# Shifting the sample caches from DRAM to DRAM in a hybrid attention layer

## The chip, the cores and the metric

The kernel runs on one core of one Trainium2 chip. The metric is device time in microseconds (us) of the whole program, as the median of its runs; lower is better. Work goes to PE (matrix products, PEld its weight loads), DVE, ACT and POOL (element-wise work), and to 16 DMA engines that move data between the core's SBUF and DRAM. DMAs are issued by two in-order instruction streams, those of SP and of ACT. ACT thus both computes and issues, and an issue that has to wait keeps all of ACT's later instructions waiting.

## The reference, cut to what matters

One inference step of a layer with three mixers (band attention A, gated delta rule B, memory attention C), a merge and a feed-forward part. Only mixer A and its caches are touched here:

```python
k_all = jnp.concatenate([cache_a_k[l], k_a], axis=1)     # 8 samples: 512 cached + 16 new keys
v_all = jnp.concatenate([cache_a_v[l], v_a], axis=1)
o_a = _band_attention(q_a, k_all, v_all, q_pos, k_pos, k_pos >= 0, a_rel_bias[l])
...
a_k_p.append(k_a[:, tp - keep_p:])    # prompt: the last 512 keys (and values) become the cache
a_k_s.append(k_all[:, tn:])           # samples: the cache moved on by 16, with the 16 new keys behind
a_v_s.append(v_all[:, tn:])
```

The sample caches hold 8 samples x 512 positions x 1024 channels in f32, 16 MB for keys and 16 MB for values. The output is almost all a copy: 496 of its 512 positions stand in the input, and 16 are new.

## The kernel before, in words

Phase A (about the first 1130 us) runs over 8 groups g of 128 channels (two heads). For each group `a_qk` projects queries and keys, `a_v` projects values (each as three chunks of 384 columns; PE, then evacuated by ACT, DVE and POOL), `a_prompt` does the band attention of the 1024 prompt frames as 4 blocks G x 2 heads h, `a_sample` that of the 8 samples in two halves hb, and `b_front` prepares mixer B. A scheduler with a simulated clock merges all of it into one list per engine, by dependences and priority, so PE alternates between projections (tile `ps`) and attention (`S`, `tb`, `od`).

The cache outputs were written as follows, all issued by ACT:

- `a_sample` loads a half's cached keys (`kb`, 1024 KB, one buffer) and values (`vb`, 1024 KB, two buffers) on SP, and from these same SBUF tiles ACT sends the shifted caches out: L450 `o_aks<-kb` (1024 KB, 128 partitions; the new keys had been copied behind the cached ones) and L451 `o_avs<-vb` (992 KB, partitions 4 to 127, thus 124 of them). Both have to wait for the load, and `kb` can't be loaded again until L450 has been sent.
- `a_v` sends the new values: L357 `o_avs<-vs`, 8 DMAs of 8 KB, one a sample, in a row.
- `a_qk` and `a_v` send the prompt caches, L317 `o_akp<-y` and L342/L344 `o_avp<-y`.

Completion is counted on 8 semaphores, called lanes below (DMAHW0 to DMAHW7 in the order rows), which go round over the DMAs of SP and ACT together. A DMA that takes a lane first waits until the DMA that had it last is complete, and that wait stands in the stream of the engine that issues it.

Of the kernel before, what the change touches and what calls it, by code (L numbers as in the profile page):

```python
# [19 lines left out]
P = 128  # L20
D = 1024
SEQ = 1024
DB = 8
DT = 16
# [4 lines left out]
MEM = 256  # L29
# [28 lines left out]
def run(g, n=-1):  # L58

    while n and next(g, g) is not g:  # L60
        n -= 1


class K:
# [219 lines left out]
    def a_qk(self, g, pool):  # L284
        nc, d, A = self.nc, self.d, self.A

        qs = [pool.tile([P, SEQ], F32R, name=f"qs{h}") for h in range(2)]
        kd = [pool.tile([P, SEQ], F32R, name=f"kd{h}") for h in range(2)]
        kl = A["kl"]
        kr = pool.tile([P, P], F32, name="kr", bufs=2)  # L290
        qb = A["qbs"][g % 2]
        A.update(qs=qs, kd=kd, krn=kr, qbn=qb)
        rows = [(slice(64 * h, 64 * h + 64), slice(64 - 64 * h, 128 - 64 * h)) for h in range(2)]

        def ev_q(c, p):
            n = slice(c * CW, min((c + 1) * CW, SEQ))
            w = n.stop - n.start
            for t, (r, o) in zip(qs, rows):
                nc.scalar.mul(t[r, n], p[r, :w], 0.125)
                nc.vector.scalar_tensor_tensor(t[o, n], p[r, :w], 0.125, t[r, n].bitcast(F32), op0=ALU.mult, op1=ALU.subtract)  # L300
            if c == 2:
                s = p[:, 256:384].rearrange("p (b i) -> p b i", b=DB)
                nc.scalar.mul(qb[0:64, :, 0:16], s[0:64], 0.125)
                nc.scalar.mul(qb[64:128, :, 16:32], s[64:128], 0.125)

        def ev_k(c, p):
            n = slice(c * CW, min((c + 1) * CW, SEQ))
            w = n.stop - n.start
            for t, low, (r, o) in zip(kd, kl, rows):
                nc.scalar.copy(t[r, n], p[r, :w])  # L310
                nc.vector.tensor_sub(low[r, n], p[r, :w], t[r, n].bitcast(F32))
                nc.gpsimd.tensor_copy(t[o, n], t[r, n].bitcast(F32))
            if c > 0:
                y = pool.tile([P, CW], F32, name="y", bufs=4)
                nc.scalar.copy(y, p)
                m = slice(128, 384) if c == 1 else slice(0, 256)
                nc.scalar.dma_start(d["o_akp"][g][:, (c - 1) * 256:c * 256], y[:, m])  # L317
            if c == 2:
                nc.gpsimd.tensor_copy(kr, y[:, 256:384])

        if g:
            self.project(g, ev_q)
            self.project(8 + g, ev_k)
        else:
            both = [self.projected(t, ev, w) for t, ev, w in zip((0, 8), (ev_q, ev_k), self.first)]
            for f in both * NCH:
                run(f, KT)
            for f in both:
                run(f)

    def a_v(self, g, pool, ps):
        nc, d, A = self.nc, self.d, self.A
        vv = pool.tile([P, 8, 2, P], F32R, name="vv")
        vs = pool.tile([P, P], F32, name="vs", bufs=2)
        oT = pool.tile([P, NT], F32, name="oT", bufs=1)
        A.update(vv=vv, vs=vs, oT=oT, kr=A["krn"], qb=A["qbn"])

        def ev_v(c, p):
            vr = pool.tile([P, CW], F32, name="y", bufs=4)
            nc.scalar.copy(vr, p)  # L340
            if c == 1:
                nc.scalar.dma_start(d["o_avp"][g][:, 0:256], vr[:, 128:384])  # L342
            if c == 2:
                nc.scalar.dma_start(d["o_avp"][g][:, 256:512], vr[:, 0:256])  # L344
            pt = ps.tile([P, 512], F32, name="pvt", tag="f")
            for i in range(3):
                self.transpose(pt[:, i * P:(i + 1) * P], in_=vr[:, i * P:(i + 1) * P], identity=self.ident)
            m = 3 if c < 2 else 2
            src = pt[:, :m * P].rearrange("p (t h e) -> p t h e", t=m, h=2)
            dst = vv[:, 3 * c:3 * c + m]  # L350
            nc.scalar.copy(dst[:, :, :, 0:64], src)
            nc.vector.tensor_sub(dst[:, :, :, 64:128], src, dst[:, :, :, 0:64].bitcast(F32))
            if c == 2:
                nc.scalar.copy(vs, pt[:, 256:384])
                dv = d["o_avs"][g][124:128]
                for b in range(DB):
                    nc.scalar.dma_start(dv[:, b, :].rearrange("p (s e) -> p s e", s=4), vs[b * 16:(b + 1) * 16, :])  # L357

        self.project(16 + g, ev_v)
        for h in range(2):  # L360

            for r, c in ((slice(0, 64), slice(0, 576)), (slice(64, P), slice(64, 640))):
                self.after_x(nc.sync.dma_start(A["tab"][h][r, c], d["btab"][2 * g + h][r, c]))
# [11 lines left out]
    def a_prompt(self, g, G, h, pool, ps):  # L375
        nc, A = self.nc, self.A
        q, k2, kl, vv, oT = A["qs"][h], A["kd"][h], A["kl"][h], A["vv"], A["oT"]
        th, tl = A["pt"][A["n"] % 2]
        A["n"] += 1
        r = slice(64 * h, 64 * h + 64)  # L380
# [10 lines left out]
        for p in (p0, p1):  # L391
# [11 lines left out]
            v = pt[:, :w].rearrange("p (i w) -> p i w", i=parts)  # L403
            tab = A["tab"][h][:, 640 - w:640].rearrange("p (i w) -> p i w", i=parts)
            self.softmax(pool, v, S[:, :parts, :pw], tab, w, "a")
            for j in range(nk):
                s = slot[(p, k0 + j)]
# [5 lines left out]
        for i in range(nb):  # L413
            m = min(2, len(full) - 2 * i)
            src = tb[i][:, :m * 256].rearrange("p (s q) -> p s q", s=m)
            s = slice(2 * i, 2 * i + m)
            nc.scalar.copy(th[:, s, :], src)
            nc.vector.tensor_sub(tl[:, s, :], src, th[:, s, :].bitcast(F32))
        e = 4 * 256 + P
        m = 256 if p0 >= 4 else P  # L420
# [3 lines left out]
        o = od[:, 0:256]  # L424
# [3 lines left out]
            self.mm(o, lhsT=vv[:, k, h, :], rhs=tl[:, s, :], start=False, stop=n == len(use) - 1)  # L428
        q = slice(64 - 64 * h, 128 - 64 * h)
        tmp = pool.tile([P, 256], F32, name="otmp", bufs=1)  # L430
        nc.scalar.copy(tmp[r], o[q])
        nc.vector.tensor_add(oT[r, G * 256:(G + 1) * 256], o[r], tmp[r])

    def a_sample(self, g, pool, ps):
        nc, d, A = self.nc, self.d, self.A
        qb, stab, kr, vs, oT = (A[n] for n in ("qb", "stab", "kr", "vs", "oT"))
        self.after_x(nc.sync.dma_start(stab, d["stab"][g]))
        for hb in range(2):
            S = ps.tile([P, 2, 512], F32, name="S", tag="s")
            bs = slice(4 * hb, 4 * hb + 4)  # L440
            kb = pool.tile([P, 4, 528], F32, name="kb", bufs=1)
            self.after_x(nc.sync.dma_start(kb[:, :, 0:512], d["cak"][g][:, bs, :]))
            nc.gpsimd.tensor_copy(kb[:, :, 512:528], kr[:, hb * 64:hb * 64 + 64].rearrange("p (b i) -> p b i", b=4))
            vb = pool.tile([P, 4, 4, P], F32, name="vb", bufs=2)
            self.after_x(nc.sync.dma_start(vb, d["cav"][g][:, bs, :].rearrange("p b (s e) -> p b s e", s=4)))
            for u in range(2):
                for i in range(4):
                    self.mm(S[32 * i:32 * i + 32, u, 0:264], lhsT=qb[:, 4 * hb + i, :], rhs=kb[:, i, u * 264:(u + 1) * 264],
                                     start=True, stop=True, tile_position=(0, 32 * i))
            nc.scalar.dma_start(d["o_aks"][g][:, bs, :], kb[:, :, 16:528])  # L450
            nc.scalar.dma_start(d["o_avs"][g][0:124, bs, :], vb[4:128].rearrange("p b s e -> p b (s e)"))  # L451
            pt = pool.tile([P, 640], F32, name="pt", bufs=2)
            self.softmax(pool, pt[:, :528].rearrange("p (i w) -> p i w", i=2), S[:, :, 0:264],
                         stab.rearrange("p (i w) -> p i w", i=2), 528, "a")
# [12 lines left out]
            r = slice(64 * hb, 64 * hb + 64)  # L467
# [5 lines left out]
            for s in range(4):  # L473
                for i in range(4):
                    q = slice(32 * i, 32 * i + 32)
# [6 lines left out]
            v = T3[:, 0:P].rearrange("p (b h i) -> p b h i", b=4, h=2)  # L482
            n0 = SEQ + 64 * hb
            for h in range(2):
                r = slice(64 * h, 64 * h + 64)
# [836 lines left out]


_OUT = {
    "o_y": (9, P, D), "o_akp": (8, P, 512), "o_avp": (8, P, 512), "o_conv": (24, P, 27), "o_ssmp": (8, P, P),
    "o_mk": (8, P, MEM), "o_mv": (8, P, MEM), "o_aks": (8, P, DB, 512), "o_avs": (8, P, DB, 512), "o_ssms": (8, P, DB * P),
}


# [43 lines left out]
def _results(r):  # L1373
    c = np.ascontiguousarray
    y = r["o_y"].reshape(NT, D)
    conv = r["o_conv"].transpose(2, 0, 1).reshape(27, 3072)
    return (
        c(y[:SEQ]).reshape(1, SEQ, D),
        c(y[SEQ:]).reshape(DB, DT, D),
        c(r["o_akp"].reshape(D, 512).T).reshape(1, 1, 512, 16, 64),  # L1380
        c(r["o_avp"].reshape(D, 512).T).reshape(1, 1, 512, 16, 64),
        c(conv[:3]).reshape(1, 1, 3, 3072),
        c(r["o_ssmp"]).reshape(1, 1, 8, P, P),
        c(r["o_mk"].reshape(D, MEM).T).reshape(1, 1, MEM, 4, 256),
        c(r["o_mv"].reshape(D, MEM).T).reshape(1, 1, MEM, 4, 256),
        c(r["o_aks"].reshape(D, DB, 512).transpose(1, 2, 0)).reshape(1, DB, 512, 16, 64),
        c(r["o_avs"].reshape(8, P, DB, 4, P).transpose(2, 1, 3, 0, 4)).reshape(1, DB, 512, 16, 64),
        c(conv[3:]).reshape(1, DB, 3, 3072),
        c(r["o_ssms"].reshape(8, P, DB, P).transpose(2, 0, 1, 3)).reshape(1, DB, 8, P, P),
    )  # L1390
# [16 lines left out]
```

## Time and profile before

| | |
|---|---|
| median of 3 runs | 2838.77 us (2837.24 to 2844.19) |
| the profiled execution | 2833.81 us, span 2832.0 us |
| busy share of the span | PE 95%, PEld 87%, DVE 51%, ACT 35%, POOL 29% |
| mean DMA rate | 121 GB/s, 343.27 MB in all |
| `o_aks<-kb`, `o_avs<-vb` | 16 issues each, 1024 and 992 KB |
| `o_avs<-vs` | 64 issues, 8 KB each |

The profile is of one execution; its own time is 5 us under the median. PE is the busiest engine, so the places where PE stands still, and where its granted clock is below 1.0, are where the time outside of matrix work is. A wait of another engine counts only if PE ends up waiting for it. In a row of the timeline, the bracket at the end is how long the engine had been idle and what the profile names as the end of it; where an instruction waited for several things, that name can be the wrong one.

### The profile page before, as it was taken

To read this page: it belongs to the slowest core of one execution; us is meant where nothing else is said; L and a number is where in the kernel's file an instruction comes from. 1 tells how busy PE (TensorE), PEld (TensorE's weight loads), DVE (VectorE), ACT (ScalarE), POOL (GpSimd) and SP (SyncE) were. 2 spreads that over 40 slices of the span, in tenths; PEclk is the share of its full clock that TensorE was granted. 3 is DMA by queue.
4 is the path that set the end of the run, shared out by engine and by line. 5 is a ranking of instruction groups with operands and counts; after the bars stand their busy time and mean duration, and the time that the engine had idled before them with its cause. 6 is when DMAs were issued, how large, how long until landed. Compare 5 with 4: busy or idle time off the path is not lost.

```text
span 2832.0 us, 45029 instructions
## 1 busy us (share of the span) xinstructions
PE 2676.8 (95%) x16361; PEld 2477.9 (87%) x16361; DVE 1446.3 (51%) x3353; ACT 1002.9 (35%) x2749; POOL 812.3 (29%) x1197
## 2 busy tenths in 40 slices
PE   8998998989898988999989898999999999999997
PEld 7988898989898987988978888888989899998986
DVE  4646373737374654333366557654545444444445
ACT  4636363736363644222333333333411111111113
POOL 2222121212131221222355555432342121121212
PEclk9999999999999999999999999999999999999999
DMA  7252525253434333444576676654201011110101
GB/s 256 77 176 72 173 75 180 73 174 100 146 119 138 121 128 112 158 170 158 173 231 184 203 199 199 195 162 146 71 30 60 30 52 38 37 53 30 52 27 67
DMA packets 263006, 343.27 MB, mean 121 GB/s; under 512 B 54704, under 2 KB 178240, under 8 KB 258752
## 3 DMA queue, kind: packets, MB, share of 16 engines
q1 hardware_dynamic: 201344, 245.93, 27.8%
q10 hardware_dynamic: 61440, 94.46, 9.6%
q8 instruction: 129, 2.11, 0.3%
q14 instruction: 93, 0.76, 0.1%
HBM read 235.18 MB, written 105.13 MB: 120 GB/s over the span
## 4 chain that ended last, share of the span: by engine, by line
PE 53%; DMA 9%; DVE 5%; issue 3%; POOL 2%; ACT 1%; SPq 0%; ACTq 0%; DVEq 0%; POOLq 0%
PE ps L115 27%; PE op L115 15%; PE t L115 2%; PE S L115 1%; PE sc L115 1%; PE od L115 1%; DMA o_avs<-vb 1%; DVE tmp L777 1%; PE kk L115 1%; PE tb L120 1%; PE o L115 1%; DMA wraw<-in_w_mem 1%; DMA o_akp<-y 1%; PE ob L115 1%; DMA vb<-in_cav 1%
## 5 line engine op out<-in xcount | busy, mean ns | idle before, releaser
L115 PE MATMUL ps<-xh,whi 128*128 128x384 f32 x2712 | 957.2, 353 | 44.2 <-ACT e L218 30.8
L115 PE MATMUL ps<-xh,wlo 128*128 128x384 f32 x2712 | 933.1, 344 | 1.3 <-DVE wlo L169 1.3
L115 PE MATMUL ps<-xl,whi 128*128 128x384 f32 x2712 | 933.6, 344 | 0.0
L115 PEld LDWEIGHTS ps<-xh,whi 128*128 128x128 f32 x2712 | 516.0, 190 | 67.3 <-ACT e L218 33.1
L115 PEld LDWEIGHTS ps<-xl,whi 128*128 128x128 f32 x2712 | 515.8, 190 | 13.4 <-issue 2.3
L115 PEld LDWEIGHTS ps<-xh,wlo 128*128 128x128 f32 x2712 | 514.5, 190 | 9.8 <-issue 2.9
L168 POOL TENSOR_SCALAR whi<-wraw 128x512 fp32r<-128x512 f32 x261 | 181.1, 694 | 470.0 <-PE ps L115 382.3
L1291 DVE TENSOR_TENSOR acc<-op,acc 128x512 f32<-128x512 f32 x252 | 174.1, 691 | 276.2 <-PE op L115 276.1
L1265 ACT ACTIVATE r<-ps,bf 128x384 f32<-128x384 f32 x96 | 55.6, 581 | 664.6 <-PE ps L115 664.6
L169 DVE TENSOR_TENSOR wlo<-wraw,whi 128x512 fp32r<-128x512 f32 x261 | 194.0, 744 | 187.0 <-POOL whi L168 179.9
L115 PE MATMUL op<-h,uh 128*128 128x512 f32 x576 | 225.5, 392 | 1.2 <-DVE sm L1295 1.2
L115 PE MATMUL op<-h,ul 128*128 128x512 f32 x576 | 226.1, 392 | 0.0
L115 PE MATMUL op<-l,uh 128*128 128x512 f32 x576 | 225.6, 392 | 0.0
L373 POOL TENSOR_SCALAR pt<-pt,sta 128x640 f32<-128x640 f32 (+3 forms) x144 | 109.4, 760 | 395.2 <-DVE sta L372 322.5
L168 POOL TENSOR_SCALAR uh<-r 128x384 fp32r<-128x384 f32 x96 | 55.5, 578 | 491.9 <-ACT r L1266 479.9
L609 DVE SCALAR_TENSOR_TENSOR y<-z,wc,y 128x384 f32<-128x384 f32 (+1 forms) x216 | 130.4, 605 | 20.9 <-ACT y L606 14.3
L115 PEld LDWEIGHTS op<-h,ul 128*128 128x128 f32 x576 | 108.2, 188 | 23.8
L371 ACT ACTIVATE pt<-pt,sta 128x640 f32<-128x640 f32 (+3 forms) x144 | 100.9, 701 | 78.3 <-DVE sta L370 31.7
L115 PEld LDWEIGHTS op<-h,uh 128*128 128x128 f32 x576 | 108.3, 188 | 19.5 <-DVE sm L1295 2.0
L369 DVE CUSTOM_DVE_ANT_0 pt<-S,tab 128x640 f32<-128x640 f32 (+4 forms) x128 | 83.5, 652 | 79.6 <-PE S L115 34.9
L115 PEld LDWEIGHTS op<-l,uh 128*128 128x128 f32 x576 | 108.1, 188 | 15.4
L169 DVE TENSOR_TENSOR ul<-r,uh 128x384 fp32r<-128x384 f32 x96 | 53.7, 560 | 102.1 <-POOL uh L168 102.1
(374 smaller groups left out, 4571.6 us busy)
## 6 DMA issues: line engine op xcount, KB each, us to landing
wraw<-in_w_in SPq DMA_DIRECT2D x160, 256.0 KB
kb<-in_cak SPq DMA_DIRECT2D x16, 1024.0 KB
vb<-in_cav SPq DMA_DIRECT2D x16, 1024.0 KB
o_aks<-kb ACTq DMA_DIRECT2D x16, 1024.0 KB
wraw<-in_w_ff SPq DMA_DIRECT2D x64, 256.0 KB
w2raw<-in_w_ff SPq DMA_DIRECT2D x64, 256.0 KB
o_avs<-vb ACTq DMA_DIRECT2D x16, 992.0 KB
spn<-kn ACTq DMA_DIRECT2D x48, 192.0 KB
```

What stands on the lines that cost most here:

```text
L115: ins = self.nc.tensor.matmul(out, **kw)
L120: ins = self.nc.tensor.transpose(out, **kw)
L168: nc.gpsimd.tensor_scalar(hi, raw, 1.0, 0.0, op0=ALU.mult, op1=ALU.add)
L169: nc.vector.tensor_sub(lo, raw, hi.bitcast(F32))
L369: nc.vector.tensor_tensor_reduce(out=P_, in0=S, in1=tab, scale=1.0, scalar=-3e38, op0=ALU.add, op1=ALU.max, accum_out=st[:, 0:1])
L371: nc.scalar.activation(P_, P_, AF.Exp, bias=st[:, 1:2], accum_out=st[:, 2:3])
L373: nc.gpsimd.tensor_scalar(P_, P_, st[:, 3:4], 0.0, op0=ALU.mult, op1=ALU.add)
L609: nc.vector.scalar_tensor_tensor(y[:, :w], z[:, i:i + w], wc[:, i:i + 1], y[:, :w], op0=ALU.mult, op1=ALU.add)
L777: nc.vector.tensor_tensor(tmp[:, 0:t, 0:t], y[:, 0:t, 0:t], m[:, 0:t, t].unsqueeze(1).broadcast_to([72, t, t]), op=ALU.mult)
L1265: nc.scalar.activation(r, p[:, :CW], AF.Relu, bias=bf[:, f:f + 1])
L1291: nc.vector.tensor_add(a, o, a)
```

## The change

The shifted part of the sample caches is copied from the input in DRAM straight to the output in DRAM, without SBUF. Each group's copy is cut into 4 parts for keys (32 channels each) and 4 for values (31 of 124 rows each), 496 KB a part. A key and a value part are issued together on ACT, just behind the copy `otmp` of the first head of each of the 4 prompt blocks (a dependence without a semaphore fixes the order). They wait for no data. The new keys and values go to arrays of their own, `o_akn` and `o_avn`, with one DMA of 64 KB each a group; prompt caches get a layout in which each DMA writes one contiguous block. The arrays are put together after the kernel.

```diff
-                nc.scalar.dma_start(d["o_akp"][g][:, (c - 1) * 256:c * 256], y[:, m])
+                nc.scalar.dma_start(d["o_akp"][g, c - 1], y[:, m])
             if c == 2:
                 nc.gpsimd.tensor_copy(kr, y[:, 256:384])
+                nc.scalar.dma_start(d["o_akn"][g], y[:, 256:384])
...
             if c == 2:
                 nc.scalar.copy(vs, pt[:, 256:384])
-                dv = d["o_avs"][g][124:128]
-                for b in range(DB):
-                    nc.scalar.dma_start(dv[:, b, :].rearrange("p (s e) -> p s e", s=4), vs[b * 16:(b + 1) * 16, :])
+                nc.scalar.dma_start(d["o_avn"][g], vs)
...
-        nc.scalar.copy(tmp[r], o[q])
+        last = nc.scalar.copy(tmp[r], o[q])
         nc.vector.tensor_add(oT[r, G * 256:(G + 1) * 256], o[r], tmp[r])
+        if h == 0:
+            self.a_shift(g, G, last.ins.name)
+
+    def a_shift(self, g, i, last):
+
+        nc, d = self.nc, self.d
+        dep = mybir.DependencyInfo(mybir.DependencyClass.NoSync, mybir.DependencyReason.DATA)
+        r = slice(32 * i, 32 * i + 32)
+        v = slice(31 * i, 31 * i + 31)
+        for ins in (nc.scalar.dma_start(d["o_aks"][g][r], d["cak"][g][r, :, 16:512]),
+                    nc.scalar.dma_start(d["o_avs"][g][v], d["cav"][g][4 + v.start:4 + v.stop])):
+            self.tc.add_manual_dep(ins.ins, last, dep, reason="shift")
...
-            nc.scalar.dma_start(d["o_aks"][g][:, bs, :], kb[:, :, 16:528])
-            nc.scalar.dma_start(d["o_avs"][g][0:124, bs, :], vb[4:128].rearrange("p b s e -> p b (s e)"))
...
-    "o_akp": (8, P, 512), "o_avp": (8, P, 512), ... "o_aks": (8, P, DB, 512), "o_avs": (8, P, DB, 512),
+    "o_akp": (8, 2, P, 256), "o_avp": (8, 2, P, 256), ... "o_aks": (8, P, DB, 496), "o_avs": (8, 124, DB, 512), "o_akn": (8, P, P), "o_avn": (8, P, P),
```

The list of every engine changes in phase A. The order of ACT before, at the end of `a_v` of group 6 (the names are tiles: `vb` the loaded values, `vs` the new values, `pth` the band's weights; a bracket names the semaphores waited for):

```order
L279 DMA oa<-oT 128x1152 [waits DMAHW5_49,DVE_49]
L451 DMA o_avs<-vb 124x2048 [waits DMAHW7_49,DMAHW3_49]
L351 CAST vv<-pvt 128x6x64 [waits PE_49]
...
L357 DMA o_avs<-vs 4x4x128 [waits Activation_49]
L357 DMA o_avs<-vs 4x4x128 [waits DMAHW4_49]
L357 DMA o_avs<-vs 4x4x128 [waits DMAHW5_49]
L357 DMA o_avs<-vs 4x4x128 [waits DMAHW6_49]
L357 DMA o_avs<-vs 4x4x128 [waits DMAHW7_49]
L357 DMA o_avs<-vs 4x4x128 [waits DMAHW0_49]
L417 CAST pth_232<-tb_9753 128x256 [waits PE_49]
```

ACT at the same place now, on to the first shift pair of the group's band (`o_aks<-in_cak` and `o_avs<-in_cav`):

```order
L279 DMA oa<-oT 128x1152 [waits DMAHW7_49,DVE_49]
L352 CAST vv<-pvt 128x6x64 [waits PE_49]
...
L416 CAST pth_232<-tb_9735 128x256 [waits PE_49]
L421 CAST pth_232<-od 128x128 [waits PE_49]
L755 DMA gb<-e 128x384 [waits DMAHW5_49,Activation_49]
L356 DMA o_avn<-vs 128x128 [waits DMAHW6_49,Activation_49]
...
L430 COPY otmp<-od 64x256 [waits PE_49]
L441 DMA o_aks<-in_cak 256x496 [waits DMAHW7_49]
L442 DMA o_avs<-in_cav 16x7936 [waits DMAHW0_49]
L755 DMA gb<-e 128x384 [waits DMAHW1_49,Activation_49]
```

The 992 KB transfer and the eight small ones (two of their rows are left out above) are gone from this place; the casts of `pth` stand ahead of the one DMA that is left, and the pair stands behind `otmp`, each of its two with a wait for a lane alone. The fifth `o_avs<-vs` had waited for the lane DMAHW7, the one that `o_avs<-vb` also names.

SP in group 6 before, around the second load of `kb` (`wraw` are weights, `stab` a bias table):

```order
L442 DMA kb<-in_cak 128x4x512 [waits DMAHW0_49,PE_49]
L176 DMA wraw<-in_w_in 128x512 [waits DMAHW1_49,DVE_49]
L176 DMA wraw<-in_w_in 128x512 [waits DMAHW6_49,DMAHW3_49,DVE_49]
L442 DMA kb<-in_cak 128x4x512 [waits DMAHW2_49,DMAHW4_49,DMAHW0_49,PE_49]
L437 DMA stab<-in_stab 128x528 [waits DMAHW5_49,DVE_49]
```

SP at the same place now:

```order
L453 DMA kb<-in_cak 128x4x512 [waits DMAHW6_49,PE_49]
L176 DMA wraw<-in_w_in 128x512 [waits DMAHW0_49,DVE_49]
L176 DMA wraw<-in_w_in 128x512 [waits DMAHW5_49,DMAHW1_49,DVE_49]
L453 DMA kb<-in_cak 128x4x512 [waits DMAHW6_49,DMAHW2_49,PE_49]
L448 DMA stab<-in_stab 128x528 [waits DMAHW3_49,DVE_49]
```

The order is the same; the second load of `kb` waits for one lane less, that on which `o_aks<-kb` was sent. Behind phase A the lists of all five engines stand as before.

## Rows read from the trace of the kernel before

**Rows 1.** The page: busy time, share and instructions of each engine.

```profile
PE 2676.8 (95%) x16361; PEld 2477.9 (87%) x16361; DVE 1446.3 (51%) x3353; ACT 1002.9 (35%) x2749; POOL 812.3 (29%) x1197
```

**Rows 2.** Busy time by stretch: first group, groups 1 to 7, all behind phase A.

```profile
core 0: us, PE busy (x) PEld busy (x) DVE busy (x) ACT busy (x) POOL busy (x), PEclk, DMA share, GB/s
...
60.00:200.00 140.00, 136.94 (x916) 130.53 (x915) 80.04 (x220) 72.56 (x199) 34.40 (x64) 1.00 0.38 127
200.00:1030.00 830.00, 768.55 (x5075) 735.72 (x5073) 449.01 (x1229) 417.95 (x1175) 194.57 (x377) 0.97 0.38 127
...
1130.00:2832.00 1702.00, 1631.15 (x9509) 1483.60 (x9508) 826.65 (x1672) 422.10 (x1146) 543.38 (x671) 0.98 0.37 114
```

**Rows 3.** Eight stretches in which PE stands still: first, last, their sum.

```profile
213.36:221.42 8.06, 0.00 (x1) 0.00 (x1) 0.60 (x3) 1.42 (x5) 0.28 (x1) 0.65 0.19 68
...
1023.51:1030.26 6.75, 0.00 (x1) 0.01 (x1) 1.02 (x4) 1.68 (x6) 0.54 (x2) 0.84 0.20 65
sum 52.49, PE 0.03 PEld 0.03 DVE 4.67 ACT 10.72 POOL 2.33; mean PE 0.00 PEld 0.00 DVE 0.58 ACT 1.34 POOL 0.29
```

**Rows 4.** The stretches at half clock behind them, PE working: first, their sum.

```profile
221.42:226.03 4.61, 4.61 (x14) 4.61 (x15) 1.85 (x4) 2.90 (x7) 1.98 (x3) 0.50 0.34 98
...
sum 36.33, PE 36.32 PEld 35.67 DVE 19.41 ACT 23.43 POOL 12.58; mean PE 4.54 PEld 4.46 DVE 2.43 ACT 2.93 POOL 1.57
```

**Rows 5.** Timeline of PE, 886 to 899 us: start, length, instruction, idle before.

```profile
894.83 0.58 PE L115 MATMUL od<-pth,vv 128*128 128x256 f32 x1 [7.45 <-DVE ptl L423]
...
895.85 0.52 PE L115 MATMUL ps<-xh,whi 128*128 128x384 f32 x1
...
898.61 0.34 PE L115 MATMUL ps<-xh,whi 128*128 128x384 f32 x1
```

**Rows 6.** Timeline of ACT, 866 to 898 us.

```profile
875.17 0.28 ACTq L451 DMA_DIRECT2D o_avs<-vb  x1
875.49 0.48 ACT L351 CAST vv<-pvt 128x384 fp32r<-128x384 f32 x1 [8.29 <-DMA vb<-in_cav]
...
880.05 13.66 ACTq L357 DMA_DIRECT2D o_avs<-vs  x7
893.75 0.37 ACT L417 CAST pth<-tb 128x256 fp32r<-128x256 f32 x1 [14.04 <-DMA o_avs<-vs]
```

**Rows 7.** Timeline of ACT, 890 to 896 us.

```profile
891.09 2.62 ACTq L357 DMA_DIRECT2D o_avs<-vs  x4
```

**Rows 8.** Waits of ACT, 0 to 1130 us: total, times, longest.

```profile
ACT pth L417 <- DMA o_avs<-vs: 27.5, 2, 14.0
ACT otmp L431 <- DMA wraw<-in_w_in: 26.9, 2, 13.6
ACT pt L371 <- DMA wraw<-in_w_in: 26.1, 2, 13.6
...
ACT otmp L431 <- DMA o_avs<-vs: 12.7, 1, 12.7
```

**Rows 9.** Four short stretches, columns as in rows 2.

```profile
74.00:84.00 10.00, 10.00 (x62) 9.31 (x61) 2.93 (x9) 2.33 (x6) 0.91 (x2) 1.00 0.13 40
734.00:742.00 8.00, 8.00 (x50) 7.95 (x50) 1.38 (x2) 0.10 (x1) 1.25 (x2) 1.00 0.56 192
881.00:890.00 9.00, 6.38 (x38) 6.03 (x36) 0.59 (x3) 0.00 (x0) 0.62 (x1) 1.00 0.24 100
970.00:974.00 4.00, 4.00 (x28) 3.96 (x26) 2.73 (x6) 1.44 (x4) 1.25 (x2) 1.00 0.77 288
```

**Rows 10.** Timeline of ACT in group 0, 74 to 82 us.

```profile
75.50 5.42 ACTq L357 DMA_DIRECT2D o_avs<-vs  x8
```

**Rows 11.** Issues that write `o_avs`: ns each, least, median, most.

```profile
L357 ACTq DMA_DIRECT2D o_avs<-vs x64: 626/629/1790, 75.5 to 1027.8; - x64
L451 ACTq DMA_DIRECT2D o_avs<-vb x16: 281/293/1585, 44.1 to 1011.0; - x16
```

**Rows 12.** Issues that write `o_aks`.

```profile
L450 ACTq DMA_DIRECT2D o_aks<-kb x16: 395/560/1642, 46.2 to 1093.4; - x16
```

More of the change, by code (lines that the diff above doesn't have):

```diff
@@ L341, in ev_v @@
             if c == 1:
-                nc.scalar.dma_start(d["o_avp"][g][:, 0:256], vr[:, 128:384])
+                nc.scalar.dma_start(d["o_avp"][g, 0], vr[:, 128:384])
             if c == 2:
-                nc.scalar.dma_start(d["o_avp"][g][:, 256:512], vr[:, 0:256])
+                nc.scalar.dma_start(d["o_avp"][g, 1], vr[:, 0:256])
             pt = ps.tile([P, 512], F32, name="pvt", tag="f")
@@ L1324 @@
 _OUT = {
-    "o_y": (9, P, D), "o_akp": (8, P, 512), "o_avp": (8, P, 512), "o_conv": (24, P, 27), "o_ssmp": (8, P, P),
-    "o_mk": (8, P, MEM), "o_mv": (8, P, MEM), "o_aks": (8, P, DB, 512), "o_avs": (8, P, DB, 512), "o_ssms": (8, P, DB * P),
+    "o_y": (9, P, D), "o_akp": (8, 2, P, 256), "o_avp": (8, 2, P, 256), "o_conv": (24, P, 27), "o_ssmp": (8, P, P),
+    "o_mk": (8, P, MEM), "o_mv": (8, P, MEM), "o_aks": (8, P, DB, 496), "o_avs": (8, 124, DB, 512), "o_akn": (8, P, P), "o_avn": (8, P, P), "o_ssms": (8, P, DB * P),
 }
@@ L1379, in _results @@
         c(y[SEQ:]).reshape(DB, DT, D),
-        c(r["o_akp"].reshape(D, 512).T).reshape(1, 1, 512, 16, 64),
-        c(r["o_avp"].reshape(D, 512).T).reshape(1, 1, 512, 16, 64),
+        c(r["o_akp"].transpose(0, 2, 1, 3).reshape(D, 512).T).reshape(1, 1, 512, 16, 64),
+        c(r["o_avp"].transpose(0, 2, 1, 3).reshape(D, 512).T).reshape(1, 1, 512, 16, 64),
         c(conv[:3]).reshape(1, 1, 3, 3072),
@@ L1385, in _results @@
         c(r["o_mv"].reshape(D, MEM).T).reshape(1, 1, MEM, 4, 256),
-        c(r["o_aks"].reshape(D, DB, 512).transpose(1, 2, 0)).reshape(1, DB, 512, 16, 64),
-        c(r["o_avs"].reshape(8, P, DB, 4, P).transpose(2, 1, 3, 0, 4)).reshape(1, DB, 512, 16, 64),
+        c(np.concatenate([r["o_aks"].reshape(D, DB, 496), r["o_akn"].reshape(D, DB, DT)], 2).transpose(1, 2, 0)).reshape(1, DB, 512, 16, 64),
+        c(np.concatenate([r["o_avs"].reshape(8, 124, DB, 4, P).transpose(2, 1, 3, 0, 4).reshape(DB, 496, 8, P),
+                           r["o_avn"].reshape(8, DB, DT, P).transpose(1, 2, 0, 3)], 1)).reshape(1, DB, 512, 16, 64),
         c(conv[3:]).reshape(1, DB, 3, 3072),
```

## The prediction

> **What bounds the kernel now.** I began with the busy shares: PE works for 95% of the span and the next engine, DVE, for 51% [rows 1]. Time can therefore leave only where PE stands still or runs below its clock, and I asked for both by stage. Phase A is the only place that the change touches; behind it all five lists stand as they did, so the 1702 us from 1130 us on are taken as unchanged. In phase A, group 0 runs with PE busy for 136.94 of 140 us and at clock 1.00, while groups 1 to 7 show 768.55 of 830 us at clock 0.97 [rows 2]. The reader is to see that the same work runs clean in group 0 and with 61.5 us of idle time in the seven groups behind.
>
> That idle time is not spread out. I listed PE's gaps: eight of them, one in each of groups 1 to 7 and one of them broken in two, hold 52.5 us together (52.49 long, 0.03 busy) [rows 3]. Their first and last lie 810.15 us apart, six groups, so a group takes 135.0 us. Right behind each comes a stretch at half clock (0.50, that is 1.2 GHz in place of 2.4): a projection product takes 0.52 us at 895.85 and 0.34 us again at 898.61 [rows 5]. Those with PE at work add up to 36.33 us [rows 4]. Work done there would have taken half the time, so 18.2 us are lost in them.
>
> Then the cause. At 894.83 PE had waited 7.45 us for `ptl` [rows 5], which DVE makes from `pth`, and ACT's cast of `pth` came at 893.75 after 14.04 us of idle time [rows 6]. ACT was standing in its own issues: seven of the `o_avs<-vs` fill 13.66 us from 880.05 [rows 6], and the last four of them begin only at 891.09 and take 2.62 us [rows 7]. So ahead of the fifth of eight ACT stood still for 6 to 9 us: the three issues since 880.05 take 0.63 to 1.79 us each [rows 11]. By the order of the change's section, that fifth waits for the lane that `o_avs<-vb` names, issued at 875.17. From 881 to 890 us, with ACT at 0.00, the DMA engines were busy for 0.24 of 16, thus 3.8 engines, and moved 100 GB/s, while a `kb` load reaches 0.77 and 288 GB/s [rows 9]. The 992 KB transfer was thus crawling on about four engines: 1.016 MB at 100 GB/s is 10.2 us, which is most of the way from 875.17 to 891.09. Seven such ACT waits, one a group, sum to 27.5 + 26.9 + 26.1 + 12.7 = 93.2 us [rows 8]; the ones labelled `wraw` end at the same kind of instruction and I read them as the same wait under a wrong name.
>
> **The change part by part.**
>
> *`o_avs<-vb` and the eight `o_avs<-vs` go.* With no four-engine transfer in flight and no eight issues to fill the lanes, the wait of 12.7 to 14.0 us in each of groups 1 to 7 goes, and with it PE's gaps: -52.5 us, and the half-clock stretches that follow them: -18.2 us. What is late next? ACT's other long wait, 8.29 us before the cast of `vv` (it stood for `o_avs<-vb`, which stood for the load of `vb`) [rows 6], goes too, and it never reached PE: in the same wait a group earlier, from 734 to 742 us, ACT did 0.10 us of work while PE was busy for 8.00 of 8.00 [rows 9]. So I book nothing for it. Group 0 shows what is left when the eight issues meet no lane wait: they take 5.42 us [rows 10], and PE is busy for 10.00 of 10.00 us around them [rows 9]. I therefore take PE's gap as gone, not as shortened.
>
> *`o_aks<-kb` goes.* The second `kb` load no longer waits for its sending. PE did not wait there in the groups' gaps, so nothing is booked; earlier loads are hidden under the band.
>
> *`o_akn`, `o_avn`, new prompt layout.* Two issues a group are added and eight go: at 0.63 us by the median [rows 11] the eight cost ACT 5.0 us a group. All this is ACT time under PE's work, with ACT busy for 418 of 830 us [rows 2]: nothing.
>
> *The 64 shift parts.* They move the bytes that went before: 4 x 496 + 4 x 496 + 64 + 64 = 4096 KB a group, as 2 x 1024 + 2 x 992 + 8 x 8 did; only the reading side is now DRAM. Each pair costs ACT two issues behind `otmp`, and behind it on ACT stand the next exponentials and casts of the band, for which PE waits in the end. No row shows a DRAM to DRAM transfer. For the issue the nearest rows are the large ones from SBUF: 0.28 us (L451, least) to 1.64 us (L450, most) [rows 11, 12], so a pair holds ACT for 0.56 to 3.3 us. From below: PE has 61.5 - 52.5 = 9.0 us of other idle time in groups 1 to 7, and if freer loads took all of it the term would be -9 us. From above: if each of 32 pairs kept PE for 3.3 us, 105 us, and the same share for the half clock as today (18.2/52.5, so a factor of 1.35), +142 us. I take 0.1 us a pair, +3 us, because holds of 5.42 us and of 8 us leave PE full in the rows just named, and a pair is shorter than either.
>
> For the transfer itself: at a `kb` load's 288 GB/s a part of 0.508 MB takes 1.8 us, at the 100 GB/s of four engines 5.1 us, 10.2 us for a pair. A group has 4 pairs in some 135 us, 34 us apart on the mean, so even the slow end leaves the lanes free long before the next pair, and mostly before eight further DMAs have gone round.
>
> How many engines a transfer gets is the place for a rule. The trace: 3.8 engines for the 124-row transfer [rows 9]. The Trainium skill, "DMA: Bandwidth & Descriptors", section "Why a DMA increments its semaphore by 16 and not by 1", says that a DMA is spread over the largest number up to 16 that divides the outermost dimension of both sides; 124 gives 4, and the trace agrees. By it a value part of 31 rows would go to a single engine, were it issued in that shape.
>
> The order rows show it as 16x7936 and the key part as 256x496, so both can be spread over 16.
>
> Sum: -52.5 - 18.2 + 3 = -67.7 us. Against the profiled execution (2833.8 us; the span and 1.8 us around it) that is 2766.1 us. The runs shown have a median 5.0 us above that execution, so on their scale 2838.8 - 67.7 = 2771 us.
>
> **The rivals.**
>
> *The wait moves (about half is kept).* The shift parts run at the slow end, 10 us a pair, and some burst of issues (the gate DMAs `gb` right behind the first pair) meets their lanes. For it: nothing in the trace shows DRAM to DRAM, and ACT is still the issuer. Against: eight DMAs have to go round first. One gap of half of today's size a group leaves -35 us: 2804 us.
>
> *No change.* PE's gap has another cause that ends at the same moment, such as weights (`wraw` is named in two of the four rows) [rows 8]. Against: group 0, the same code without the lane wait, has no gap. 2839 us.
>
> *Slower: the pairs stall the band.* ACT issues a pair between two steps of a softmax chain, 32 times, at the long issues of 1.6 us, and PE has nothing else at hand there. It decides from 70.7/(32 x 1.35) = 1.6 us of PE gap a pair on; at 3.3 us, +142 - 71 = +71 us: 2910 us. For it: L450's 1.64 us and L451's 1.59 us occur, and the second of a pair always follows another large issue. Against: 5.42 us of ACT hold in group 0 cost PE nothing.
>
> *Slower: a value part on one engine.* 0.508 MB at 100/3.8 = 26 GB/s is 19.5 us, 78 us a group on one engine through which all other transfers pass too. With four gaps a group of the size of today's one, the loss is 3 x 70.7 = +212 us: 3051 us. The rule named above would do this to 31 rows; the shape in the order speaks against it.
>
> **How the numbers follow.** Forecast, gaps gone (2759 to 2790): 0.73. The wait moves (2790 to 2815): 0.14. No change: 0.04. Pairs stall the band: 0.07. One engine: 0.02. The low end is the sum with the -9 us bound in place of +3, 2838.8 - 79.7 = 2759; the high end is the half-kept case, 2803. About 0.82 lies inside. What a measurement of this kernel can tell from no change is about 0.3%, 8.5 us. Faster by more than that: forecast and moved wait, 0.87. Within it: 0.05, which is no change and a little of the third case. Slower: 0.08.
>
> **What would show it.** Right: in groups 1 to 7 no PE gap over 2 us, clock 1.00 there, the distance between the same step of two groups down from 135.0 to about 125 us, no ACT wait over 6 us named for a DMA, and everything behind phase A as long as before. The new issues should take 0.3 to 0.6 us each; the DMA share during a shift should be well over 4 of 16. Wrong: gaps of 1 us and more behind the `otmp` copies, half-clock stretches at the pairs, or waits of ACT for lanes of shift parts.

## The result, and the profile after

| | before | changed |
|---|---|---|
| median of the runs | 2838.01 us (4 runs) | 2750.14 us (4 runs, 2741.3 to 2760.32) |
| ratio | | 0.969, 95% interval 0.9651 to 0.9729 |
| the profiled execution | 2833.81 us | 2752.38 us |

The kernel became 3.1% faster, 88 us by the medians and 81.4 us by the two profiled executions. The forecast was 2771 us with a range of 2759 to 2803: the direction was right and the gain was larger than the range allowed.

Busy shares on the page after, as in [rows 1]:

```profile
PE 2655.3 (97%) x16361; PEld 2464.2 (90%) x16361; DVE 1448.3 (53%) x3353; ACT 1004.5 (37%) x2749; POOL 809.3 (29%) x1197
```

Busy time by stretch after, columns as in [rows 2], which it answers (group 0, groups 1 to 7, a shift pair of group 3, all behind phase A):

```profile
60.00:200.00 140.00, 135.21 (x896) 127.84 (x894) 78.69 (x218) 70.92 (x198) 31.83 (x63) 0.99 0.36 120
200.00:963.00 763.00, 763.00 (x5173) 738.89 (x5172) 466.59 (x1261) 433.70 (x1216) 199.92 (x389) 1.00 0.42 140
501.00:505.00 4.00, 4.00 (x26) 4.00 (x25) 2.86 (x7) 3.13 (x7) 1.17 (x3) 1.00 0.87 284
1048.00:2750.50 1702.50, 1630.61 (x9511) 1482.09 (x9509) 823.98 (x1673) 422.08 (x1146) 541.62 (x671) 0.98 0.37 114
```

In groups 1 to 7 PE is busy for 763.00 of 763.00 us at clock 1.00, where it had been idle for 61.5 us [rows 2]: all of the idle time is gone, the eight gaps [rows 3] and the 9.0 us beside them, and no half-clock stretch [rows 4] is left there. A group takes 122.6 us (the copy `vs<-pvt` of groups 1 and 7 starts at 205.7 and 941.3 us), where the prediction expected about 125. Group 0 did not gain: PE is busy for 135.21 us there in place of 136.94, with a short stretch at half clock (0.99 on the mean). Behind phase A the last 1702 us are as before. The first copy from DRAM to DRAM that a row shows runs in a stretch with 0.87 of the DMA engines busy and 284 GB/s, other transfers of those 4 us included.

ACT at the end of `a_v` of group 7 after, the place that [rows 6] show in group 6 (start, length, instruction, idle before):

```profile
940.99 0.37 ACT L416 CAST pth<-tb 128x256 fp32r<-128x256 f32 x1 [0.40 <-PE tb L120]
941.26 0.27 ACT L355 COPY vs<-pvt 128x128 f32<-128x128 f32 x1
941.42 0.29 ACT L421 CAST pth<-od 128x128 fp32r<-128x128 f32 x1
941.56 0.34 ACTq L356 DMA_DIRECT2D o_avn<-vs  x1
...
946.67 0.37 ACT L430 COPY otmp<-od 64x256 f32<-64x256 f32 x1 [0.45 <-PE od L115]
946.68 0.55 ACTq L441 DMA_DIRECT2D o_aks<-in_cak  x1
947.27 0.61 ACTq L442 DMA_DIRECT2D o_avs<-in_cav  x1
```

The cast of `pth` had come after 14.04 us of ACT idle time in group 6; here it is 0.40. One issue of 0.34 us stands for eight, and a pair holds ACT for 1.2 us.

For the stage alone I use one mark, the first store of the memory keys (`o_mk`), which is the first thing of the next phase. It is the first start time in these rows (ns least/median/most, first and last start), of before and of after:

```profile
L1030 ACTq DMA_DIRECT2D o_mk<-mr x8: 344/344/364, 1155.3 to 1330.8; - x8
```

```profile
L1039 ACTq DMA_DIRECT2D o_mk<-mr x8: 344/344/367, 1073.6 to 1248.1; - x8
```

So phase A gave 81.7 us, which is the whole of the difference of the two executions: from the mark to the end of the span it is 1676.7 us before and 1676.9 us after.

### The profile page after: what moved, and what is told of

Same layout as the page of the kernel before. It is cut to its first block, busy times and chain, and to the rows that moved or that the text cites. A ratio compares the mean times of both kernels' runs of the same rounds, so it can differ in the third digit from the quotient of the medians.

```text
span 2750.5 us, 45013 instructions
## 1 busy us (share of the span) xinstructions
PE 2655.3 (97%) x16361; PEld 2464.2 (90%) x16361; DVE 1448.3 (53%) x3353; ACT 1004.5 (37%) x2749; POOL 809.3 (29%) x1197
## 4 chain that ended last, share of the span: by engine, by line
PE 81%; DMA 8%; DVE 5%; issue 3%; POOL 2%; ACT 1%; SPq 0%; ACTq 0%; DVEq 0%; POOLq 0%
PE ps L115 48%; PE op L115 16%; PE od L115 3%; PE S L115 3%; PE t L115 2%; PE tb L120 2%; PE sc L115 1%; PE tp L120 1%; PE kk L115 1%; DMA bv<-spn 1%; DVE tmp L786 1%; PE o L115 1%; DMA wraw<-in_w_mem 1%; PE ob L115 1%; DMA kb<-in_cak 1%
```

## The experiments

"Mark" is the start of that first store in each run's own profile, thus of one execution a run; the changed kernel's three profiles lie 2.0 us apart (1073.6 to 1075.6), and before has one profile alone. The medians also hold the stages behind the mark, and one of those, the delta rule's, differed by up to 16 us between runs (see e8 and e10). e1, e2, e3 and e6 ran on another chip than the rest; the medians of before there were 2836.87 and 2841.05 us.

One thing the edits hide: the scheduler merges the lists of the engines anew for each kernel. By the traces, e2 runs the instructions of phase A in the order of the kernel before, and e4, e5 and e9 in that of the changed kernel. e1, e3, e6, e7 and e8 (e10 is the same kernel) each have another order on every engine that computes, so what they differ by can be the edit or the order.

| run | what it is | median us | ratio, 95% interval | mark us | against before |
|---|---|---|---|---|---|
| e1 | before, one DMA of new values | 2763.89 | 0.9734, 0.9706 to 0.9762 | 1077.3 | -78.0 |
| e2 | before, value transfer of 128 rows | 2765.28 | 0.974, 0.9713 to 0.9767 | 1083.2 | -72.1 |
| e3 | change, eight DMAs of new values | 2767.82 | 0.9748, 0.9716 to 0.978 | 1084.6 | -70.7 |
| e6 | change, every part copied twice | 2772.8 | 0.9765, 0.9729 to 0.9801 | 1101.6 | -53.7 |
| e4 | the change again | 2752.06 | 0.969, 0.9668 to 0.9711 | 1075.2 | -80.1 |
| e9 | the change, third time | 2752.05 | 0.9688, 0.9667 to 0.971 | 1075.6 | -79.7 |
| e5 | change, value parts of 31 rows | 3018.26 | 1.0623, 1.0597 to 1.0649 | 1336.8 | +181.5 |
| e7 | change, a group's shift at once | 2777.89 | 0.9771, 0.9737 to 0.9805 | 1089.9 | -65.4 |
| e8 | change, shift issued by SP | 2758.17 | 0.9726, 0.9698 to 0.9754 | 1069.3 | -86.0 |
| e10 | the same as e8 | 2760.12 | 0.9712, 0.9692 to 0.9733 | 1070.1 | -85.2 |

**e1: only the eight small DMAs go.**

```diff
-                dv = d["o_avs"][g][124:128]
-                for b in range(DB):
-                    nc.scalar.dma_start(dv[:, b, :].rearrange("p (s e) -> p s e", s=4), vs[b * 16:(b + 1) * 16, :])
+                nc.scalar.dma_start(d["o_avn"][g], vs)
```

> The kernel before, with one edit: the eight 8 KB DMAs of the new values are one of 64 KB to an array of its own; the caches still leave from SBUF, the value transfer still with 124 rows. Lane theory (PE's gap came from the fifth of the eight small DMAs waiting for the lane of the 992 KB transfer that crawls on about four DMA engines): with one small DMA the lanes do not come round, the 12.7 to 14 us wait of ACT goes and the 70.7 us with it: about 2768 us, and some 15 us above the change, since ACT's 8 us wait for the load of the cached values stays. Rival 1 (the crawling transfer hurts by itself, through the weights that share its engines): most of the gap stays, over 2805 us. Rival 2 (all of the gain comes from the lane wait): as fast as the change, about 2750 us.

2763.89 us, with the 992 KB transfer of 124 rows still in place. Rival 1 falls: with one small DMA in place of eight, the slow transfer no longer costs PE much. Waits for it are still there, on SP, whose stream computes nothing (total, times, longest, up to the mark):

```profile
SPq L584 <- DMA o_avs<-vb: 71.6, 8, 11.4
```

At the mark e1 has 78.0 of the change's 81.7 us. The expected 15 us above the change did not show in phase A, where it is 1.7 to 3.7 us; the median is 11.8 us above e4, but the delta rule's stage took 531.0 us in e1's profile and 518.8 in e4's. So Rival 2 is close to the truth for phase A.

**e2: only the slow transfer goes.**

```diff
-            nc.scalar.dma_start(d["o_avs"][g][0:124, bs, :], vb[4:128].rearrange("p b s e -> p b (s e)"))
+            nc.scalar.dma_start(d["o_avs"][g][:, bs, :], vb.rearrange("p b s e -> p b (s e)"))
...
-                dv = d["o_avs"][g][124:128]
+                dv = d["o_avx"][g]
```

> The kernel before, with the value transfer given 128 rows in place of 124 (the four rows too many are dropped after the kernel) and the eight small DMAs kept, to an array of their own. Lane theory: 128 rows are spread over all 16 engines, the transfer is over in about 4 us in place of 15, the fifth small DMA finds its lane free, and the eight issues take about 5.4 us as in group 0, which PE does not notice: about 2768 us. Rival (the eight issues are the cost, or ACT's wait for the loads): stays within 10 us of 2838.

2765.28 us. ACT in group 6 of e2, timeline as above:

```profile
816.03 0.34 ACTq L451 DMA_DIRECT2D o_avs<-vb  x1
...
823.95 0.65 ACTq L357 DMA_DIRECT2D o_avx<-vs  x1
824.64 4.62 ACTq L357 DMA_DIRECT2D o_avx<-vs  x7
829.30 0.37 ACT L417 CAST pth<-tb 128x256 fp32r<-128x256 f32 x1 [4.99 <-DMA o_avx<-vs]
```

The stretch behind that issue, in which two loads of weights are in flight beside the transfer, and PE under the eight issues (columns as in [rows 2]):

```profile
817.00:821.00 4.00, 4.00 (x27) 3.96 (x26) 1.73 (x6) 1.56 (x4) 1.00 (x2) 1.00 0.99 341
824.00:830.00 6.00, 6.00 (x38) 5.93 (x37) 1.20 (x6) 1.01 (x5) 0.38 (x1) 1.00 0.04 11
```

With four more rows, the stretch behind the transfer's issue has 0.99 of the engines busy and 341 GB/s in place of 0.24 and 100 GB/s [rows 9], and the seven issues take 4.62 us in place of 13.66 [rows 6]. With e1 this settles the cause: it took the slow transfer and the eight DMAs together, and either one taken away frees ACT. What e2 gains at the mark, 72.1 us, is the slow transfer and the waits for it, with the order of all lists unchanged. In no group of e2 does PE have a gap within 20 us behind the first of the eight issues. Its waits from 200 to 980 us (total, times, longest):

```profile
PE od L115 <- DVE ptl L423: 2.9, 2, 1.4
PE S L115 <- DVE sta L369: 2.6, 4, 0.7
```

Both lie elsewhere; they come back in the part on the prediction.

**e3: the eight DMAs put back into the change.**

```diff
-                nc.scalar.dma_start(d["o_avn"][g], vs)
+                dv = d["o_avx"][g]
+                for b in range(DB):
+                    nc.scalar.dma_start(dv[:, b, :].rearrange("p (s e) -> p s e", s=4), vs[b * 16:(b + 1) * 16, :])
```

> The changed kernel, with the eight 8 KB DMAs of the new values put back in place of the one of 64 KB. Lane theory: no slow transfer holds a lane, so eight issues cost ACT 5 us a group and PE nothing: within 6 us of the change, 2744 to 2758. Rival (the eight issues are the cost): 35 us or more slower than the change, over 2785.

Neither: 2767.82 us, 15.8 above e4 (the delta rule's stage has 5.8 of them, 524.6 us against 518.8), and 9.0 to 11.0 us later at the mark than the change's three profiles. ACT and PE in e3 behind the eight issues of group 1 (two timelines):

```profile
205.56 5.42 ACTq L358 DMA_DIRECT2D o_avx<-vs  x8
211.08 0.37 ACT L432 COPY otmp<-od 64x256 f32<-64x256 f32 x1 [5.38 <-PE S L115]
211.11 0.60 ACTq L443 DMA_DIRECT2D o_aks<-in_cak  x1
211.75 0.62 ACTq L444 DMA_DIRECT2D o_avs<-in_cav  x1
```

```profile
215.01 0.33 PE L120 MATMUL tb<-cst,pt 128*128 128x128 f32 x1 [1.58 <-POOL pt L374]
```

The eight issues hold ACT for 5.42 us, the pair right behind them for 1.3 more, and PE waits 1.58 us. PE's waits from 200 to 980 us in e3:

```profile
PE tb L120 <- POOL pt L374: 4.7, 3, 1.6
PE od L115 <- DVE ptl L424: 2.9, 2, 1.4
PE S L115 <- DVE sta L370: 1.2, 2, 0.6
```

The first of them is the wait just shown. It occurs in groups 1, 4 and 6, the three in which a pair stands right behind the eight issues; in the other four of groups 1 to 7 PE has no gap within 20 us behind the first of them. The other two are away from the issues, as in e2. PE's busy time in groups 1 to 7 of e3, of e2 and of e1 (200 to 980 us, columns as before):

```profile
200.00:980.00 780.00, 770.34 (x5194) 743.40 (x5193) 463.00 (x1270) 435.91 (x1220) 208.93 (x395) 1.00 0.42 137
```

```profile
200.00:980.00 780.00, 774.14 (x5212) 746.67 (x5211) 467.27 (x1281) 437.16 (x1223) 203.41 (x396) 1.00 0.41 137
```

```profile
200.00:980.00 780.00, 777.97 (x5226) 744.97 (x5225) 474.43 (x1291) 438.68 (x1241) 210.19 (x398) 1.00 0.42 138
```

9.7 and 5.9 us idle with eight issues, 2.0 with one, 0.0 in the change. But only 4.7 us of it stand at the issues, all of them in e3: a hold of 5 us by itself was free there and in e2, and one that a pair lengthens to 6.8 us cost PE 1.6 us.

**e6: every part copied a second time.**

```diff
+                    nc.scalar.dma_start(self.twice_k[g][r], d["cak"][g][r, :, 16:512]),
+                    nc.scalar.dma_start(self.twice_v[g][v], d["cav"][g][4 + v.start:4 + v.stop])):
```

> The changed kernel, with every shift part copied a second time to a scratch array in DRAM, so twice the shift issues on ACT and 32 MB more to move. What I had booked for the pairs (0.1 us each, 3 us in all) says about 2753; if pairs cost nothing at all, 2750. The rival that pairs stall the band would show as a cost for the second set: 20 us or more, with PE gaps behind the first-head copies. If the DMA engines are near their limit, weights come late and it is over 2790.

2772.8 us, 20.7 above e4, and 26.0 to 28.0 us at the mark. Waits of PE in phase A of e6 (total, times, longest):

```profile
PE S L115 <- DMA kb<-in_cak: 14.0, 6, 3.6
PE S L115 <- DVE sta L370: 12.6, 12, 2.6
```

The cost has the size that the rival named, but not its place: the largest wait was neither for ACT behind the first-head copies nor for weights but for the load of `kb`. So a second set of parts is not free, at a share of 0.51 of the DMA engines in groups 1 to 7 where the change has 0.42. That the extra copies make the load late is the likely reading; the order of the lists changed too.

**e5: value parts of 31 rows.**

```diff
-                    nc.scalar.dma_start(d["o_avs"][g][v], d["cav"][g][4 + v.start:4 + v.stop])):
+                    nc.scalar.dma_start(d["o_avs"][g][v, 0:4096], d["cav"][g][4 + v.start:4 + v.stop].rearrange("p b e -> p (b e)"))):
...
-    ... "o_avs": (8, 124, DB, 512), ...
+    ... "o_avs": (8, 124, 4112), ...
```

> The changed kernel, with each value part issued as 31 rows of 16 KB (the output rows get a pad, so that they can't be merged) in place of 16 of 31 KB; the same bytes. By the shape rule of the prediction's rival, 31 rows go to one DMA engine: about 20 us a part at 26 GB/s, all striped weight and cache loads wait on that engine, lanes are held for longer than eight DMAs take to come round, and PE's gaps are back: over 2800 us, with ACT waits named for DMAs. If shape does not matter: within 8 us of the change.

3018.26 us: the same bytes, cut into 31 rows, make the kernel 6% slower than before, with every list in the changed kernel's order. A stretch of e5 (columns as before) and PE's wait at its end:

```profile
580.00:590.00 10.00, 4.29 (x26) 3.93 (x24) 0.00 (x0) 0.00 (x0) 0.00 (x0) 0.82 0.07 27
```

```profile
592.54 0.63 PE L115 MATMUL S<-kd,qs 128*128 128x320 f32 x1 [8.25 <-DVE sta L368]
```

0.07 of 16 is one engine, at 27 GB/s, with ACT at a stand. The prediction's rival of one engine (3051 us) was real, and the shape in the order, 16x7936, is what kept it away.

**e7: a group's shift at once.**

```diff
-        if h == 0:
+        if h == 0 and G == 0:
...
-        r = slice(32 * i, 32 * i + 32)
-        v = slice(31 * i, 31 * i + 31)
+        r = slice(0, P)
+        v = slice(0, 124)
```

> The changed kernel, with a group's whole shift (1984 KB of keys, 1984 KB of values, both over 16 engines) issued at once behind the first block's first head, in place of four pairs along the band. Theory: 4 MB at some 380 GB/s are 11 us of DMA time once a group, and the eight DMAs behind it do not come round in that time: PE loses little, 2750 to 2765. Rival (the parts along the band are what makes the change work): the two hold their lanes and delay the gate DMAs and weights, gaps of several us a group come back, over 2785.

2777.89 us, between the two: 13 us over what the theory allowed and short of the rival's 2785. ACT waits 25.5 us for `gb` DMAs and PE has gaps of 2 to 3.6 us in four groups. At the mark e7 is 14 to 16 us behind the change, and its delta rule's stage took 530.8 us, 11 to 12 us more than the change's. The 14 to 16 us are what cutting along the band is worth, with the lists in another order.

**e4 and e9: the change again.**

> The changed kernel once more, in more rounds, since its first runs lay between 2741 and 2760. If the profiled execution stands for it (PE idle for 0.0 us in groups 1 to 7, 81.7 us gained by the end of phase A, nothing behind it): 2750 to 2757, a gain of 80 to 87 us. If the change also gains behind phase A: under 2747. If the first runs were lucky and my sum was right: 2765 or more.

> The changed kernel, on one chip beside the next one. Its two profiles so far end phase A (first store of the memory keys) at 1073.6 and 1075.2 us, 81.7 and 80.1 us ahead of before. Expected: 1073 to 1076 there, 2748 to 2756 in all.

2752.06 and 2752.05 us: the gain is 88 to 89 us by the medians of before that were taken beside them (2841.05, 2839.61), 80 us by the marks. The profile behind before's mark lies near the low end of before's runs; where its other runs lose up to 15 us more is not known.

**e8 and e10: the shift issued by SP.**

```diff
-        for ins in (nc.scalar.dma_start(d["o_aks"][g][r], d["cak"][g][r, :, 16:512]),
-                    nc.scalar.dma_start(d["o_avs"][g][v], d["cav"][g][4 + v.start:4 + v.stop])):
+        for ins in (nc.sync.dma_start(d["o_aks"][g][r], d["cak"][g][r, :, 16:512]),
+                    nc.sync.dma_start(d["o_avs"][g][v], d["cav"][g][4 + v.start:4 + v.stop])):
```

> The changed kernel, with the shift parts issued by SP in place of ACT. The changed kernel's pairs hold ACT for 1.2 us each, 4.6 us a group, and eight small issues in a row (5.4 us) cost PE about 1.4 us a group in the run that put them back. If ACT's hold by the pairs costs PE anything: up to 10 us faster than the change. Since PE has no idle time left in groups 1 to 7, I expect no gain: within 5 us. Rival: SP's stream of weight loads is held up by the shift's lane waits, and it is 10 us or more slower.

> The shift parts issued by SP, again, on the same chip as the changed kernel. The first profile ended phase A at 1069.3 us, 4 to 6 us ahead of the changed kernel, and then lost 10 us in the delta rule's stage, whose length has varied by as much among kernels with the same instructions there. If the pairs' hold of ACT is a real cost: phase A at 1068 to 1071 again, and some 5 us faster in all when the later stage does not hide it. If that was chance: phase A at 1073 or more.

Phase A is shorter both times, 1069.3 and 1070.1 us at the mark, 3.5 to 6.3 us ahead of the change. In all it is not faster: 2758.17 and 2760.12 against 2752. The delta rule's stage, from the first `dat<-at` to the first `mg<-og`, takes 529.6 and 534.4 us there, and 518.8 to 519.5 in the change's three profiles, with the same instructions in the same order. It isn't a better version. In groups 1 to 7 there was nothing to gain; what e8 has more of is in group 0, where PE is busy for 137.60 us at clock 1.00 (the change: 135.21 and 0.99):

```profile
60.00:200.00 140.00, 137.60 (x921) 131.17 (x920) 80.11 (x220) 72.15 (x199) 34.10 (x64) 1.00 0.39 130
```

## Why the prediction was wrong

**The bound, its cause and its size were right.** PE's gaps came from ACT's lane wait for the 992 KB transfer: taking away either partner frees it (e1, e2). The term -52.5 - 18.2 = -70.7 us measured -72.1 in e2, where only the transfer's engines changed. This is not luck: the lists being the same, the two traces can be laid side by side, product by product, and the seven places of the gaps give 72.3 us while all other differences cancel out. That the half-clock stretches go with the gaps was right too: 1.00 in groups 1 to 7.

**The step that failed: 9.0 us of other idle time were left standing, at nothing.** The prediction saw that PE was idle for 61.5 us in groups 1 to 7 and that its gaps held 52.5 of them. It used the other 9.0 us only as a bound from below, and did not ask what they consisted of. All of it went: 763.00 of 763.00 us. PE's waits of the kernel before from 200 to 1030 us (a fifth, `ps` for ACT's `e`, lies in the gaps) say what it was:

```profile
PE od L115 <- DVE ptl L423: 17.2, 4, 7.5
PE ps L115 <- ACT y L340: 2.8, 3, 2.1
PE S L115 <- DVE sta L369: 2.6, 4, 0.7
PE pvt L120 <- DVE vv L352: 2.1, 2, 1.1
```

- 2.1 us for `vv` and 0.7 for `y` (its other 2.1 are one of the eight gaps) stand behind ACT's wait for the load of the cached values. The prediction said that this wait never reached PE, on the strength of one group in which PE was full from 734 to 742 us. A gap of 0.37 us begins there at 742.5, just behind that window, and three more stand at the same place in other groups. These 2.8 us go in e2, with the slow transfer.
- 2.9 us of `od` (the other 14.4 are two of the gaps) and 2.6 of `S` stay in e2 to the tenth, and go in the change. They begin some 70 us behind the eight issues, while ACT computes. e6 has the eight issues no longer, and one pair of the same waits all the same (timeline of PE in e6):

```profile
784.95 0.42 PE L115 MATMUL S<-kd,qs 128*128 128x320 f32 x1 [0.60 <-DVE sta L370]
787.25 0.39 PE L115 MATMUL od<-pth,vv 128*128 128x256 f32 x1 [1.45 <-DVE ptl L424]
```

So these 5.5 us hang on the order in which the lists were merged and not on a hold of ACT. The change's section says that every list changes, and the sum has no term for it. Whether it was taking out the eight issues that brought the better order (e3 has such waits, e1 none) is not shown: no run has the changed kernel's order with the eight issues, or the order of before without them.

**The eight issues.** The prediction put their 5.0 us of ACT under PE's work, after group 0, where PE was full for 10.00 of 10.00 us. As a statement on the hold this was right: PE has no gap at them in any group of e2. Yet the kernel with the eight put back, e3, reaches the mark 9.0 to 11.0 us later than the change. 4.7 us of that are the three places where a pair lengthens the hold, which did not exist before; 4.1 are the waits of the order.

**The pairs.** +3 us was booked, and in groups 1 to 7 PE stands at no pair. But group 0 has 1.7 us more idle time than before and a stretch at half clock. e8 and e10, which take the pairs off ACT, gain 3.5 to 6.3 us in phase A and have neither, so the sign may have been right. Their lists have another order and the parts wait in SP's stream, so the figure is for the move and not for the pairs alone. The fear that pairs stall the band in every group was wrong.

The steps at the mark: -72.1 (e2), +1.4 from e2 to e3 (the transfers come from DRAM in pairs instead of from SBUF, and the order changes), -9.0 to -11.0 from e3 to the change; -79.7 to -81.7 in all, against -67.7 predicted.

**The scale.** I moved the sum from the profiled execution to the median of before by adding 5.0 us. The profile of before lay at the low end of its runs (2832 to 2849 over all of them), while the change's profile lay 2.2 us above the median of its first runs. Of the 21 us between 2771 and 2750.14, 14 are the sum (2766.1 against 2752.4) and 7 are this step. Measured from execution to execution, 2833.8 - 81.4 = 2752.4, the lower bound was 2833.8 - 79.7 = 2754, still above it.

**The rivals.** The moved wait, no change and the stalled band did not come; the single engine came as soon as the shape allowed it (e5). No rival was for a gain larger than the sum's.

## What to carry to other kernels

A DMA that runs on few engines is cheap as long as nobody waits for it, and it becomes dear when a burst of small DMAs comes round to its completion semaphore, on an engine that also computes: read the rows of outermost dimensions (124, 31 against 128, 16) and count the DMAs behind a slow one. Small idle time that remains beside a named cause belongs into the sum with a guess of its own: list those waits one by one. One clean stretch shows that a wait can be free, not that it is in every group. Where a scheduler merges the lists anew, compare the order before a difference is put down to the edit; of the edits here, e2 and e5 alone kept the order, so that what they changed is the edit's alone.

## What the runs showed of the hardware

- Copies from DRAM to DRAM of 496 KB ran about as fast as loads: 284 GB/s at 0.87 of the engines in a stretch with two in flight, against 288 GB/s at 0.77 in one with a `kb` load [rows 9], all transfers of the stretch counted. By the median, issuing one costs ACT 0.54 us for keys (256 rows) and 0.62 us for values (16 rows), against 0.29 us for a 124-row transfer from SBUF [rows 11].
- The number of rows went with the rate: 31 rows 27 GB/s, 124 rows 100 GB/s, 128 rows 341 GB/s in their stretches, the last with two loads of weights beside it.
- A wait for the slow transfer's lane cost PE a gap in each of groups 1 to 7 when it stood on ACT, which also computes. In e1 it stood on SP, for 71.6 us in all, and PE was idle for 2.0 of 780 us.
- The stage of the delta rule took 518.6 to 534.4 us in kernels that have the same instructions there in the same order; why is open. No run was made for it.
